# LayerNorm in one decoder layer: the variance by one 264-column product with the ones matrix, the inverse root on all copies, the last scalings in quarters

## The chip, the cores and the metric

The kernel runs on one NeuronCore of one Trainium2 chip. Its engines work side by side, each through a queue of its own in order: TensorE (PE) multiplies matrices, with its weight loads (PEld) listed beside it; VectorE (DVE) and ScalarE (ACT) do elementwise work; GpSimd (POOL) and SyncE (SP) do small jobs and issue DMAs. The metric is device time in microseconds (us), lower is better. Before the change it is 2132.67 us, the median of three runs (2131.72 to 2135.8).

## The reference

One layer with post-LayerNorm residuals over 1056 tokens (1024 of a prompt, 32 of samples), each with 1024 features:

```
h = LN1(alpha*x + 0.5*SwiGLU_a(x))
z = h @ w_in + b_in                      # attention, spatial gating and gates from z
h = LN2(alpha*h + (sigmoid(gA)*(A@w_oa) + sigmoid(gB)*(B@w_ob)) @ w_out)
y = LN3(alpha*h + 0.5*SwiGLU_b(h))

def layer_norm(x, g, b):
    mu = mean(x); var = mean((x - mu)**2)
    return (x - mu) * rsqrt(var + 1e-5) * g + b
```

All is float32. Only the three LayerNorms LN1, LN2 and LN3 are touched here. The kernel works with x/alpha in place of x, so its constant beside the variance is EPL = 1e-5/alpha^2.

## The kernel before

**Layout.** Activations lie transposed: a tile has 128 features on its partitions and tokens along its columns. The tokens are cut into four chunks of C = 264 columns, c0 to c3. A chunk of a LayerNorm's input is held in two tiles Y[c][0] and Y[c][1] of 4 x 264 columns (128x1056), so 8 feature blocks in all. A float32 product is done as three passes on split operands (high by high, high by low, low by high); all of them are issued from line 243, in the helper `mm3`.

**What comes into a norm.** Each feature block of a chunk is a residual sum that ends in a product of 12 passes (LN1 and LN3) or 24 passes (LN2) into one of three PSUM banks called mm. DVE evicts the bank and adds it to Y: line 1155 in LN1 and LN3 (function `out`), line 2025 in LN2 (function `mix`). A bank can be filled again only when DVE has evicted it; so TensorE is at most three blocks ahead of DVE.

**A norm of one chunk, before.** `center` takes the mean: line 761 multiplies the ones matrix (1/1024 everywhere, so the sum comes out on all 128 partitions) with a 264-column sum of the blocks, and line 767 subtracts it from the two tiles, 1056 columns each. `square_step` squares a block on ACT (line 806) and adds pairs on DVE (line 810). `norm` then does, for LN1, LN2 and LN3:

- line 816 adds the last two 264-column sums (DVE); line 819 brings the variance into a 128x3 tile, tokens on partitions: three products with one column each, weights the sums (PE, six passes in the trace);
- ACT takes the square root of the 128x3 tile (line 876); DVE the reciprocal and a Newton step (lines 877 to 880). For c3 of LN2 and c2 of LN3 all of it is done on DVE with three Newton steps (lines 867 to 872);
- after HOP[i] steps of the generator, line 833 spreads the result over all partitions: three products with the identity (PE, six passes);
- line 844 multiplies the two tiles by it (DVE, 128x1056 each), line 852 applies gain and bias (ACT, eight blocks of 264 columns; in c3 every second block is done by DVE, line 849). LN1 and LN2 then split the result into high and low parts (lines 254 and 255) for the next stage's products; LN3 sends it out by DMA (line 858).

**What sets the order.** A list scheduler places every instruction at build time, by priorities and by its own estimates of duration. Evictions and squares are marked `urgent` (300 places ahead). The norms are generators in a queue that `tick` advances after each block of products; `yield` and `pause(n)` hand back to it, so HOP sets after how many steps a norm goes on. Each engine then runs its list in that order, and a waiting instruction holds all behind it on its engine.

Of the kernel before, what the change touches and what calls it, by code (L numbers as in the profile page):

```python
# [12 lines left out]
F32 = mybir.dt.float32  # L13
F32R = mybir.dt.float32r
I32 = mybir.dt.int32
AF = mybir.ActivationFunctionType
ALU = mybir.AluOpType
# [4 lines left out]
P = 128  # L22
# [5 lines left out]
C = 264  # L28
NC = NT // C
KH = KB // 2  # L30
# [13 lines left out]
EPS = 1e-5  # L44
EPL = EPS / ALPHA**2
# [17 lines left out]
ROWS = 8  # L63
LATE = 16
MID = 3
HOP = (4, 1, 4)
WARM = 2
MAGIC = float(0x5F3759DF)
BOTH = mybir.DependencyInfo(mybir.DependencyClass.Sync, mybir.DependencyReason.DATA)
# [15 lines left out]
class Trunk:  # L85
# [631 lines left out]
    def consts(self):  # L717
        nc, a, cp = self.nc, self.a, self.cp
        self.ident = cp.tile([P, P], F32, name="ident")
        make_identity(nc, self.ident)  # L720
        self.eps = {}
        for e in (EPS, EPL):
            self.eps[e] = cp.tile([P, 1], F32, name=f"eps{len(self.eps)}")
            nc.vector.memset(self.eps[e], e)
        self.ones = cp.tile([P, P], F32, name="ones")
        nc.vector.memset(self.ones, 1.0 / D)
        self.cols = cp.tile([P, 98], F32, name="cols")
        nc.sync.dma_start(self.cols, a["cols"])
        self.qb = cp.tile([P, 6], F32, name="qb")
        nc.vector.tensor_scalar(self.qb, self.cols[:, 48:54], -0.125, None, op0=ALU.mult)  # L730
# [54 lines left out]
    def square_step(self, c, n, tail=False):  # L785

        nc = self.nc
        tt = nc.vector.tensor_tensor
# [3 lines left out]
        sq = self.sq  # L792
        if tail:
# [6 lines left out]
            else:  # L800
                with self.urgent():
                    tt(sq[:, 0], y, y, op=ALU.mult)
                    tt(s[:, 0], s[:, 0], sq[:, 0], op=ALU.add)
            return
        with self.urgent():
            nc.scalar.activation(sq[:, n % 2], y, AF.Square)
# [4 lines left out]

    def norm(self, c, i, mode, Y, s):
        nc = self.nc
        offs = (0, P, C - P)
        if mode != "out" or c < NC - 1:
            nc.vector.tensor_tensor(s[:, 0], s[:, 0], s[:, 1], op=ALU.add)
        pv = self.ax_tile()[:, :3]
        for j, o in enumerate(offs):
            nc.tensor.matmul(pv[:, j : j + 1], s[:, 0, o : o + P], self.ones[:, 0:1], start=True, stop=True)  # L819
        rt = self.X([P, 2, 3], "rs")  # L820
        r, t = rt[:, 0], rt[:, 1]
        if c == NC - 1 and i == 1 or c == NC - 2 and mode == "out":
            self.rsqrt_dve(r, t, self.X([P, 3], "rx", 1), pv, EPL)
        else:
            self.rsqrt(r, t, pv, EPL)
        if i == 1 and c == NC - 2:
            nc.scalar.activation(self.X([P, 2], "warm", 1)[:, :1], r[:, :1], AF.Silu)
        for _ in range(HOP[i]):
            yield
        pb = self.ax_tile()[:, :C]  # L830
        for j, o in enumerate(offs):
            lo = 0 if j < 2 else 2 * P - o
            nc.tensor.matmul(  # L833
                pb[:, o + lo : o + P], r[:, j : j + 1].to_broadcast([P, P]), self.ident[:, lo:], start=True, stop=True
            )
        yield
        while mode == "out" and c == NC - 2 and NC - 1 not in self.lns:
            yield
# [2 lines left out]
        cast = None  # L841
        for j in range(2):
            y = Y[j]
            nc.vector.tensor_tensor(y, y, pb.unsqueeze(1).to_broadcast([P, KH, C]), op=ALU.mult)  # L844
            for m in range(KH):
                n = KH * j + m
                g, b = self.vec(2 * i, n), self.vec(2 * i + 1, n)
                if c == NC - 1 and m % 2:
# [22 lines left out]
            tt(t, t, -0.5, r, op0=ALU.mult, op1=ALU.mult)  # L871
            self.chain = tt(r, t, 1.5, r, op0=ALU.add, op1=ALU.mult).ins

    def rsqrt(self, r, t, v, eps):
        tt = self.nc.vector.scalar_tensor_tensor
        self.nc.scalar.activation(r, v, AF.Sqrt, bias=self.eps[eps])
        self.nc.vector.reciprocal(r, r)
        tt(t, v, eps, r, op0=ALU.add, op1=ALU.mult)
        tt(t, t, -0.5, r, op0=ALU.mult, op1=ALU.mult)
        self.chain = tt(r, t, 1.5, r, op0=ALU.add, op1=ALU.mult).ins  # L880

    def start_ln(self, c, i, mode):
        g = self.norm(c, i, mode, self.Y[c], self.sqs[c])
# [1339 lines left out]
```

## Time and profile before

The profiled execution took 2133.41 us, with a span of 2130.2 us on the core; 3.2 us lie around the span. The median of the runs shown is 0.74 us below the profiled execution.

| what | value |
|---|---|
| median of three runs | 2132.67 us |
| profiled execution / its span | 2133.41 / 2130.2 us |
| PE busy | 2100.3 us (99%) |
| DVE busy | 1590.1 us (75%) |
| ACT busy | 935.4 us (44%) |
| granted TensorE clock, mean | 0.995 |

LN1 lies at about 650 to 702 us of the span, LN2 at about 1380 to 1490, LN3 at about 2040 to the end. A row of the timeline gives the start, the time to the end of the last of its instructions, engine, line, operation, the tile written and the tiles read, the number of instructions, and in brackets the idle time of the engine before it with what ended it. Since instructions of an engine overlap at their ends, the rate of a run of equal ones is read from the starts of two rows, not from one row's length. The rows of windows give: window, its length, then busy time (and count) of PE, PEld, DVE, ACT and POOL, then the granted clock, the DMA engines' mean busy share and GB/s.

### The profile page before, as it was taken

Reading aid. Unit: us, or ns where it says so; the run is one execution under the profiler, and the core shown is the slowest. Engines: PE = TensorE matmul, PEld = TensorE weight load, DVE = VectorE, ACT = ScalarE, POOL = GpSimd, SP = SyncE. Lnnn points to the kernel's source line nnn. Section 1 sums busy time; section 2 is a strip of 40 time slices with the busy share of each in tenths; the row PEclk is TensorE's granted clock in tenths of the full one; section 3 lists DMA queues with packets and bytes.
Section 4 is the critical chain, followed back from the end, with each engine's and each line's share of the span. In section 5 each row is a group of like instructions: output and inputs, shape, how many; then the busy total and the mean of one; then the engine's idle time right before and its main releaser. Section 6 shows DMA issues by size and latency. Waiting matters only on the chain.

```text
span 2130.2 us, 43357 instructions
## 1 busy us (share of the span) xinstructions
PE 2100.3 (99%) x17163; PEld 2066.2 (97%) x17163; DVE 1590.1 (75%) x2918; ACT 935.4 (44%) x1894; POOL 394.2 (19%) x374
## 2 busy tenths in 40 slices
PE   9999999999999999999999999999999999999997
PEld 8999999999999999999988889999999999999997
DVE  8877777766789846888767568787777777757787
ACT  5554454432224644434476543164545545512224
POOL 0234334300000022323001130000443333300000
PEclk9999999999999999999999999999999999999998
DMA  4365565499984336676855666332546545598752
GB/s 153 112 214 176 172 227 184 164 372 356 320 327 175 127 132 212 223 248 222 287 195 175 190 207 202 123 121 96 167 174 212 195 141 181 197 367 308 294 182 82
DMA packets 172187, 437.54 MB, mean 205 GB/s; under 512 B 23600, under 2 KB 58096, under 8 KB 169296
## 3 DMA queue, kind: packets, MB, share of 16 engines
q1 hardware_dynamic: 169568, 430.37, 57.3%
q0 software_dynamic: 1984, 3.87, 0.8%
q8 instruction: 134, 2.20, 0.4%
q10 hardware_dynamic: 432, 0.54, 0.1%
q14 instruction: 69, 0.57, 0.1%
HBM read 315.32 MB, written 165.57 MB: 226 GB/s over the span
## 4 chain that ended last, share of the span: by engine, by line
PE 95%; DVE 3%; DMA 1%; issue 1%; ACT 0%; POOL 0%; ACTq 0%; DVEq 0%
PE ax L243 51%; PE mm L243 39%; PE ax L1437 1%; PE ax L1487 1%; PE ax L1464 1%; DVE W L255 1%; DVE S L255 0%; DVE S L844 0%; DMA S<-cD 0%; PE ax L833 0%; PE mm L1860 0%; DMA S<-xc 0%; DVE S L767 0%; PE ax L1420 0%; PE ax L819 0%
## 5 line engine op out<-in xcount | busy, mean ns | idle before, releaser
L243 PE MATMUL ax<-S,W 128*128 128x264 f32 x7392 | 988.6, 284 | 1.8 <-DVE W L255 1.8
L243 PEld LDWEIGHTS ax<-S,W 128*128 128x128 f32 x7392 | 936.2, 188 | 2.6 <-DVE W L255 2.5
L243 PE MATMUL mm<-S,W 128*128 128x264 f32 x5232 | 735.8, 287 | 8.8 <-ACT S L254 2.7
L243 PEld LDWEIGHTS mm<-S,W 128*128 128x128 f32 x5232 | 674.1, 189 | 22.3 <-issue 6.5
L243 PE MATMUL mm<-S,S 128*128 128x264 f32 x1944 | 284.8, 285 | 3.8 <-DVE S L1155 2.4
L243 PEld LDWEIGHTS mm<-S,S 128*128 128x128 f32 x1944 | 255.3, 188 | 5.9 <-issue 2.3
L254 ACT CAST W<-R 128x512 fp32r<-128x512 f32 (+4 forms) x214 | 137.5, 658 | 230.8 <-DMA R<-w2pa 65.7
L255 DVE TENSOR_TENSOR W<-R,W 128x512 fp32r<-128x512 f32 (+4 forms) x214 | 178.3, 837 | 60.8 <-ACT W L254 59.1
L243 PE MATMUL ax<-S,S 128*128 128x264 f32 x1488 | 219.0, 284 | 0.2 <-DVE S L1048 0.2
L243 PEld LDWEIGHTS ax<-S,S 128*128 128x128 f32 x1488 | 196.7, 188 | 0.5 <-DVE S L1048 0.4
L255 DVE TENSOR_TENSOR W<-Q,W 128x512 fp32r<-128x512 f32 (+2 forms) x199 | 147.7, 759 | 56.8 <-ACT W L254 56.8
L254 ACT CAST W<-Q 128x512 fp32r<-128x512 f32 (+2 forms) x199 | 128.7, 678 | 106.6 <-DVE Q L393 104.5
L1048 DVE SCALAR_TENSOR_TENSOR S<-ax,S 128x264 f32<-128x264 f32 x240 | 99.4, 427 | 60.8 <-PE ax L243 59.6
L111 POOL CAST S<-ones 128x1 fp32r<-128x1 f32 x36 | 12.8, 364 | 583.5 <-PE ax L243 210.8
L612 ACT ACTIVATE S<-S 128x528 f32<-128x528 f32 x80 | 47.2, 638 | 135.6 <-DVE S L609 135.6
L446 POOL TENSOR_TENSOR Q<-R 128x512 f32<-128x512 f32 x36 | 47.4, 1315 | 200.9 <-DVE W L255 86.9
L474 POOL TENSOR_TENSOR Q<-R 128x256 f32<-128x256 f32 x20 | 20.7, 1034 | 344.2 <-DVE W L255 273.1
L255 DVE TENSOR_TENSOR S<-Q,S 128x1024 fp32r<-128x1024 f32 (+1 forms) x59 | 65.6, 1111 | 22.5 <-ACT S L254 22.4
L1264 ACT ACTIVATE S<-ax,cols 128x264 f32<-128x264 f32 (+5 forms) x99 | 40.3, 496 | 90.6 <-PE ax L243 86.3
L652 DVE TENSOR_TENSOR M<-M,M 128x264 f32<-128x264 f32 x60 | 63.4, 1082 | 11.7 <-ACT M L658 11.7
L254 ACT CAST S<-Q 128x1024 fp32r<-128x1024 f32 (+1 forms) x59 | 56.9, 965 | 31.9 <-DVE Q L404 29.0
L600 ACT COPY M<-ax 128x264 f32<-128x264 f32 x80 | 26.9, 376 | 95.0 <-issue 88.1
(269 smaller groups left out, 2326.4 us busy)
## 6 DMA issues: line engine op xcount, KB each, us to landing
ws<-st SPq DMA_DIRECT2D x144, 256.0 KB
S<-sumsA SPq DMA_DIRECT2D x63, 528.0 KB
S<-sumsB SPq DMA_DIRECT2D x63, 528.0 KB
R<-w13b SPq DMA_DIRECT2D x54, 512.0 KB
R<-w13a SPq DMA_DIRECT2D x52, 512.0 KB
M<-kv SPq DMA_DIRECT2D x96, 256.0 KB
sumsA<-M SPq DMA_DIRECT2D x90, 264.0 KB
sumsB<-M SPq DMA_DIRECT2D x90, 264.0 KB
```

Of the source, the lines that this page charges most:

```text
L243: mm = lambda a, b, s, e: nc.tensor.matmul(o, a[:, cc], b, start=s, stop=e, skip_group_check=True)
L254: a = self.nc.scalar.copy(hi, src)
L255: b = self.nc.vector.tensor_tensor(lo, src, hi.bitcast(F32), op=ALU.subtract)
L446: tt(s12[:, lo], cd[:, lo], cd[:, hi], op=ALU.add)
L600: go(one, 1, lambda x: copy(r[:, x], one[x]), True)
L612: nc.scalar.activation(h[:, x], h[:, x], AF.Silu)
L652: nc.vector.tensor_tensor(t, t, m, op=ALU.add)
L1048: nc.vector.scalar_tensor_tensor(y(x, r, e), bank[x], HALF, y(x, r, e), op0=ALU.mult, op1=ALU.add)
L1264: nc.scalar.activation(o, view(bank[x]), fn, bias=b, scale=sc)
L1437: m = nc.tensor.matmul(pS[h][:, r, :nk], q[e, i * P : (i + 1) * P], k[e, k0 : k0 + nk], start=True, stop=True)
L1464: nc.tensor.transpose(pT[r][:, h, o], s[:, r, h, o], self.ident)
L1487: nc.tensor.matmul(pv[0][e, (i % 4) * P : (i % 4 + 1) * P], V[:, i - (nb - 1) + b, e], sT[:, r, h, b * P : b * P + P], start=b == 0, stop= ...
```

## The change

For every norm but c3 of LN2, which keeps the way on 128x3 tiles (three products out, the root on DVE, three products back; now a function `narrow_root`):

- DVE forms -s0-s1 in place of s0+s1 (line 819 in the new numbering), and one product of the ones matrix with that 264-column tile gives minus the variance on all 128 partitions at once (line 820). The product back is gone.
- after HOP[i] steps, now (2, 1, 2) in place of (4, 1, 4), `wide_root` works on 128x264 elements: ACT takes the inverse root r of 4(var+EPL) from PSUM (line 870) and 4r^2 (line 871), DVE does two operations in place in PSUM (lines 874 and 875), a Newton step. LN2's c2 loads the Silu table behind it, as before (line 873).
- the scaling (now line 835) stands inside the loop over blocks; for c2 and c3 of LN3 it is done in four pieces of 128x528, each just ahead of the two blocks that read it, in place of two of 128x1056.
- one constant tile of 4*EPL takes the place of two.

```diff
@@ -63,7 +63,7 @@
 ROWS = 8
 LATE = 16
 MID = 3
-HOP = (4, 1, 4)
+HOP = (2, 1, 2)
 WARM = 2
 MAGIC = float(0x5F3759DF)
 BOTH = mybir.DependencyInfo(mybir.DependencyClass.Sync, mybir.DependencyReason.DATA)
@@ -718,10 +718,8 @@
         nc, a, cp = self.nc, self.a, self.cp
         self.ident = cp.tile([P, P], F32, name="ident")
         make_identity(nc, self.ident)
-        self.eps = {}
-        for e in (EPS, EPL):
-            self.eps[e] = cp.tile([P, 1], F32, name=f"eps{len(self.eps)}")
-            nc.vector.memset(self.eps[e], e)
+        self.eps = cp.tile([P, 1], F32, name="eps")
+        nc.vector.memset(self.eps, 4 * EPL)
         self.ones = cp.tile([P, P], F32, name="ones")
         nc.vector.memset(self.ones, 1.0 / D)
         self.cols = cp.tile([P, 98], F32, name="cols")
@@ -800,7 +798,9 @@
             else:
                 with self.urgent():
                     tt(sq[:, 0], y, y, op=ALU.mult)
-                    tt(s[:, 0], s[:, 0], sq[:, 0], op=ALU.add)
+                    nc.vector.scalar_tensor_tensor(
+                        s[:, 0], s[:, 0], -1.0, sq[:, 0], op0=ALU.mult, op1=ALU.subtract
+                    )
             return
         with self.urgent():
             nc.scalar.activation(sq[:, n % 2], y, AF.Square)
@@ -811,28 +811,15 @@
 
     def norm(self, c, i, mode, Y, s):
         nc = self.nc
-        offs = (0, P, C - P)
-        if mode != "out" or c < NC - 1:
-            nc.vector.tensor_tensor(s[:, 0], s[:, 0], s[:, 1], op=ALU.add)
-        pv = self.ax_tile()[:, :3]
-        for j, o in enumerate(offs):
-            nc.tensor.matmul(pv[:, j : j + 1], s[:, 0, o : o + P], self.ones[:, 0:1], start=True, stop=True)
-        rt = self.X([P, 2, 3], "rs")
-        r, t = rt[:, 0], rt[:, 1]
-        if c == NC - 1 and i == 1 or c == NC - 2 and mode == "out":
-            self.rsqrt_dve(r, t, self.X([P, 3], "rx", 1), pv, EPL)
+        if c == NC - 1 and i == 1:
+            pb = yield from self.narrow_root(s)
         else:
-            self.rsqrt(r, t, pv, EPL)
-        if i == 1 and c == NC - 2:
-            nc.scalar.activation(self.X([P, 2], "warm", 1)[:, :1], r[:, :1], AF.Silu)
-        for _ in range(HOP[i]):
-            yield
-        pb = self.ax_tile()[:, :C]
-        for j, o in enumerate(offs):
-            lo = 0 if j < 2 else 2 * P - o
-            nc.tensor.matmul(
-                pb[:, o + lo : o + P], r[:, j : j + 1].to_broadcast([P, P]), self.ident[:, lo:], start=True, stop=True
-            )
+            pb = self.ax_tile()[:, :C]
+            if mode != "out" or c < NC - 1:
+                nc.vector.scalar_tensor_tensor(s[:, 0], s[:, 0], -1.0, s[:, 1], op0=ALU.mult, op1=ALU.subtract)
+            nc.tensor.matmul(pb, self.ones, s[:, 0], start=True, stop=True)
+            yield from self.pause(HOP[i])
+            self.wide_root(pb, i == 1 and c == NC - 2)
         yield
         while mode == "out" and c == NC - 2 and NC - 1 not in self.lns:
             yield
@@ -841,8 +828,11 @@
         cast = None
         for j in range(2):
             y = Y[j]
-            nc.vector.tensor_tensor(y, y, pb.unsqueeze(1).to_broadcast([P, KH, C]), op=ALU.mult)
+            q = KH // 2 if mode == "out" and c >= NC - 2 else KH
             for m in range(KH):
+                if m % q == 0:
+                    e = y[:, m : m + q]
+                    nc.vector.tensor_tensor(e, e, pb.unsqueeze(1).to_broadcast([P, q, C]), op=ALU.mult)
                 n = KH * j + m
                 g, b = self.vec(2 * i, n), self.vec(2 * i + 1, n)
                 if c == NC - 1 and m % 2:
@@ -871,13 +861,38 @@
             tt(t, t, -0.5, r, op0=ALU.mult, op1=ALU.mult)
             self.chain = tt(r, t, 1.5, r, op0=ALU.add, op1=ALU.mult).ins
 
-    def rsqrt(self, r, t, v, eps):
-        tt = self.nc.vector.scalar_tensor_tensor
-        self.nc.scalar.activation(r, v, AF.Sqrt, bias=self.eps[eps])
-        self.nc.vector.reciprocal(r, r)
-        tt(t, v, eps, r, op0=ALU.add, op1=ALU.mult)
-        tt(t, t, -0.5, r, op0=ALU.mult, op1=ALU.mult)
-        self.chain = tt(r, t, 1.5, r, op0=ALU.add, op1=ALU.mult).ins
+    def wide_root(self, v, silu):
+
+        nc = self.nc
+        m = self.M([P, 2, C])
+        r, q = m[:, 0], m[:, 1]
+        tt = nc.vector.scalar_tensor_tensor
+        nc.scalar.activation(r, v, AF.Abs_reciprocal_sqrt, bias=self.eps, scale=-4.0)
+        nc.scalar.activation(q, r, AF.Square, scale=2.0)
+        if silu:
+            nc.scalar.activation(self.X([P, 2], "warm", 1)[:, :1], q[:, :1], AF.Silu)
+        tt(v, v, EPL, q, op0=ALU.subtract, op1=ALU.mult)
+        self.chain = tt(v, v, 3.0, r, op0=ALU.add, op1=ALU.mult).ins
+
+    def narrow_root(self, s):
+
+        nc = self.nc
+        nc.vector.tensor_tensor(s[:, 0], s[:, 0], s[:, 1], op=ALU.add)
+        offs = (0, P, C - P)
+        pv = self.ax_tile()[:, :3]
+        for j, o in enumerate(offs):
+            nc.tensor.matmul(pv[:, j : j + 1], s[:, 0, o : o + P], self.ones[:, 0:1], start=True, stop=True)
+        rt = self.X([P, 2, 3], "rs", 1)
+        r = rt[:, 0]
+        self.rsqrt_dve(r, rt[:, 1], self.X([P, 3], "rx", 1), pv, EPL)
+        yield
+        pb = self.ax_tile()[:, :C]
+        for j, o in enumerate(offs):
+            lo = 0 if j < 2 else 2 * P - o
+            nc.tensor.matmul(
+                pb[:, o + lo : o + P], r[:, j : j + 1].to_broadcast([P, P]), self.ident[:, lo:], start=True, stop=True
+            )
+        return pb
 
     def start_ln(self, c, i, mode):
         g = self.norm(c, i, mode, self.Y[c], self.sqs[c])
```

Old and new line numbers of the lines that stay: 1155 becomes 1170, 767 becomes 765, 761 becomes 759, 757/758 become 755/756, 844 becomes 835, 852 becomes 842, 849 becomes 839, 797 and 798/799 become 795 and 796/797, 802/803 become 800/801; 806, 810, 254 and 255 stay.

In the rows below S names tiles of activations or weights, M and X the middle-sized and small ones, mm and ax PSUM banks; the tile written stands left of the arrow. In LN1 the halves of c0, c1, c2, c3 are S_5567/S_5976, S_5697/S_5978, S_5569/S_5980, S_5699/S_5982 before, and after the change S_5565/S_5974, S_5695/S_5976, S_5567/S_5978, S_5697/S_5980.

**DVE in LN1, while c2's blocks come in.** Before, from the second of c2's evictions to its fifth:

```order
L1155 SCALAR_TENSOR_TENSOR S_5569<-mm_8540,S_5569 128x264
L816 TENSOR_TENSOR M_8330<-M_8330 128x264
L1155 SCALAR_TENSOR_TENSOR S_5569<-mm_8555,S_5569 128x264
L1155 SCALAR_TENSOR_TENSOR S_5569<-mm_8580,S_5569 128x264
L844 TENSOR_TENSOR S_5567<-S_5567,ax_8380 128x1056
L844 TENSOR_TENSOR S_5976<-S_5976,ax_8380 128x1056
L810 TENSOR_TENSOR M_8527<-M_8527,M_8569 128x528
L767 TENSOR_TENSOR S_5699<-S_5699,ax_8389 128x1056
L767 TENSOR_TENSOR S_5982<-S_5982,ax_8389 128x1056
L877 RECIPROCAL X_8534<-X_8534 128x3
L1155 SCALAR_TENSOR_TENSOR S_5980<-mm_8604,S_5980 128x264
```

The scaling of c0 (844) and the subtraction of c3's mean (767) stand between the fourth and the fifth. After, from the second mean subtraction of c2 on:

```order
L765 TENSOR_TENSOR S_5978<-S_5978,ax_8304 128x1056
L755 TENSOR_TENSOR M_8335<-M_7931 128x264
L255 TENSOR_TENSOR W_9304<-R_9265,W_9303 128x1024
L1170 SCALAR_TENSOR_TENSOR S_5976<-mm_8443,S_5976 128x264
L810 TENSOR_TENSOR M_8328<-M_8328,M_8378 128x528
L756 TENSOR_TENSOR M_8335<-M_8335,S_7395 128x264
L874 SCALAR_TENSOR_TENSOR ax_8330<-ax_8330,M_8352 128x264
L1170 SCALAR_TENSOR_TENSOR S_5976<-mm_8459,S_5976 128x264
L1170 SCALAR_TENSOR_TENSOR S_5567<-mm_8504,S_5567 128x264
L810 TENSOR_TENSOR M_8328<-M_8328,M_8425 128x528
L875 SCALAR_TENSOR_TENSOR ax_8330<-ax_8330,M_8352 128x264
L1170 SCALAR_TENSOR_TENSOR S_5567<-mm_8523,S_5567 128x264
```

and right behind these:

```order
L765 TENSOR_TENSOR S_5697<-S_5697,ax_8388 128x1056
L765 TENSOR_TENSOR S_5980<-S_5980,ax_8388 128x1056
L810 TENSOR_TENSOR M_8328<-M_8328,M_8457 128x528
L835 TENSOR_TENSOR S_5565<-S_5565,ax_8330 128x1056
L835 TENSOR_TENSOR S_5974<-S_5974,ax_8330 128x1056
L1170 SCALAR_TENSOR_TENSOR S_5567<-mm_8548,S_5567 128x264
```

The same four wide operations now stand two evictions earlier in c2, between its second (mm_8523) and third (mm_8548).

**PE at the same place.** Before, from the end of c2's fourth block:

```order
L243 MATMUL mm_8580<-S_8033,W_8130 128x264
L833 MATMUL ax_8380<-ident,X_8337 128x128 x2
L833 MATMUL ax_8380<-ident,X_8337 128x8
L761 MATMUL ax_8389<-M_8345,ones 128x264
L819 MATMUL ax_8530<-ones,M_8330 128x1 x3
L243 MATMUL mm_8604<-S_7955,S_8162 128x264
```

After, from the end of c2's second block:

```order
L243 MATMUL mm_8523<-S_8032,W_8078 128x264
L243 MATMUL mm_8523<-S_8031,W_8079 128x264
L759 MATMUL ax_8388<-M_8335,ones 128x264
L243 MATMUL mm_8548<-S_7953,W_8127 128x264
L243 MATMUL mm_8548<-S_7954,W_8127 128x264
```

The small products of 833 and 819 are gone from here; c3's mean product stands alone between two blocks. (A float32 product of the ones matrix or the identity is one row here and two matmuls in the trace.)

**ACT at the end of LN3.** S_23045/S_23452 are c2's halves and S_23175/S_23454 c3's before; S_22994/S_23401 and S_23124/S_23403 after. Before:

```order
L797 ACTIVATE M_26133<-S_23454 128x264
L876 ACTIVATE X_26170<-ax_26166,eps_165 128x3
L852 ACTIVATE S_23045<-S_23045,cols 128x264 x4
L852 ACTIVATE S_23452<-S_23452,cols 128x264 x4
L852 ACTIVATE S_23175<-S_23175,cols 128x264 x2
L852 ACTIVATE S_23454<-S_23454,cols 128x264 x2
```

After:

```order
L871 ACTIVATE M_25971<-M_25971 128x264
L795 ACTIVATE M_26054<-S_23403 128x264
L842 ACTIVATE S_22994<-S_22994,cols 128x264 x2
L870 ACTIVATE M_26091<-ax_26089,eps 128x264
L842 ACTIVATE S_22994<-S_22994,cols 128x264 x2
L842 ACTIVATE S_23401<-S_23401,cols 128x264 x2
L871 ACTIVATE M_26091<-M_26091 128x264
L842 ACTIVATE S_23401<-S_23401,cols 128x264 x2
L842 ACTIVATE S_23124<-S_23124,cols 128x264 x2
L842 ACTIVATE S_23403<-S_23403,cols 128x264 x2
```

Before, c3's root stands ahead of all of c2's gain-and-bias steps; after, its two ACT steps (870 and 871) stand behind two and behind six of them.

## The prediction

> **What bounds the kernel now.** I read the page's head and chain first, then windows over the three norms, then the timelines of those windows.
>
> ```profile
> span 2130.2 us, 43357 instructions
> PE 2100.3 (99%) x17163; PEld 2066.2 (97%) x17163; DVE 1590.1 (75%) x2918; ACT 935.4 (44%) x1894; POOL 394.2 (19%) x374
> PE 95%; DVE 3%; DMA 1%; issue 1%; ACT 0%; POOL 0%; ACTq 0%; DVEq 0%
> ```
>
> The chain that ended last is TensorE for 95%. Whatever leaves TensorE's list ought to shorten the end one for one, unless another engine is late just there. So the stages of the norms must be seen by themselves (LN1, a piece of LN2, LN3, the tail):
>
> ```profile
> 655.00:700.00 45.00, 42.48 (x340) 41.61 (x339) 42.23 (x77) 24.46 (x47) 0.00 (x0) 1.00 0.32 109
> 1380.00:1450.00 70.00, 70.00 (x579) 69.87 (x578) 58.62 (x97) 39.12 (x70) 1.72 (x6) 1.00 0.27 98
> 2060.00:2095.00 35.00, 34.85 (x281) 34.38 (x279) 30.55 (x57) 11.88 (x26) 0.00 (x0) 1.00 0.02 6
> 2115.00:2131.00 16.00, 2.92 (x18) 2.80 (x18) 7.89 (x18) 6.56 (x13) 0.00 (x0) 0.58 0.34 136
> ```
>
> In LN1 DVE is busy 42.23 of 45.00 us, and TensorE 42.48: two engines are at their limit, and TensorE already waits. In LN2 TensorE is busy throughout and DVE has 11 us free of 70. In LN3 DVE is at 87%. In the last 16 us TensorE hardly works: a serial tail.
>
> **What leaves TensorE.** The price of the small products stands between rows of the stream in LN2:
>
> ```profile
> 1427.45 11.13 PE L243 MATMUL mm<-S,W 128*128 128x264 f32 x90
> 1438.42 0.72 PE L819 MATMUL ax<-ones,M 128*128 128x1 f32 x6
> 1439.00 8.24 PE L243 MATMUL mm<-S,W 128*128 128x264 f32 x66
> 1447.08 0.73 PE L833 MATMUL ax<-ident,X 128*128 128x128 f32 x6
> 1447.67 24.31 PE L243 MATMUL mm<-S,W 128*128 128x264 f32 x198
> 655.52 0.60 PE L761 MATMUL ax<-M,ones 128*128 128x264 f32 x2
> 655.77 1.82 PE L243 MATMUL mm<-S,W 128*128 128x264 f32 x12
> ```
>
> Start to start, 90 passes take 10.97, so 0.122 each and 1.466 for a block of 12. Line 819 takes 1439.00 - 1438.42 = 0.58, line 833 0.59. The new product has the form of line 761, which takes 655.77 - 655.52 = 0.25 (two passes at 0.122). One norm loses 0.58 + 0.59 - 0.25 = 0.92. In the stream this counts for four chunks in LN1 (3.7), three in LN2 (2.8) and two in LN3 (1.8); of LN3's c2 only line 819 and the new product lie in the stream (0.34). Sum 8.6 us off TensorE.
>
> [...]
>
> **What it costs on DVE and ACT.** Out go a reciprocal and three 128x3 operations of 0.16; in come two operations of 128x264 on PSUM. On ACT a 128x3 root becomes two of 264 columns.
>
> ```profile
> L1048 DVE SCALAR_TENSOR_TENSOR S<-ax,S 128x264 f32<-128x264 f32 x240 | 99.4, 427 | 60.8 <-PE ax L243 59.6
> L806 ACT ACTIVATE M<-S 128x264 f32<-128x264 f32 x94 | 36.7, 419 | 65.8 <-DVE S L1155 31.5 <-DVE S L2025 22.5 <-DVE S L767 11.7
> L767 DVE TENSOR_TENSOR S<-S,ax 128x528 f32<-128x528 f32 x8 | 5.2, 697 | 0.1
> L876 ACT ACTIVATE X<-ax,eps 128x3 f32<-128x3 f32 x10 | 2.6, 259 | 5.9 <-PE ax L819 5.9
> ```
>
> In place in PSUM was not in the trace. Its nearest row, line 1048 (reads PSUM, 264 columns), gives 0.43, 0.35 from start to start; I take that, 0.16 as lower bound (the small operations) and 0.70 (twice the elements) as upper. DVE so gains a few tenths per norm and no more. The new ACT functions I price at line 806's 0.42 (bounds 0.26 and 0.84); ACT is busy 24.46 of LN1's 45 us and hides that.
>
> **LN1: the order counts more than the price.**
>
> ```profile
> 675.24 0.61 PE L761 MATMUL ax<-M,ones 128*128 128x264 f32 x2
> 676.04 2.40 DVE L767 TENSOR_TENSOR S<-S,ax 128x1056 f32<-128x1056 f32 x2
> 678.37 1.21 DVE L255 TENSOR_TENSOR W<-R,W 128x1024 fp32r<-128x1024 f32 x1
> 685.07 0.73 PE L833 MATMUL ax<-ident,X 128*128 128x128 f32 x6
> 685.65 0.69 PE L761 MATMUL ax<-M,ones 128*128 128x264 f32 x2
> 685.84 2.42 DVE L844 TENSOR_TENSOR S<-S,ax 128x1056 f32<-128x1056 f32 x2
> 686.18 0.72 PE L819 MATMUL ax<-ones,M 128*128 128x1 f32 x6
> 688.17 0.70 DVE L810 TENSOR_TENSOR M<-M,M 128x528 f32<-128x528 f32 x1
> 688.79 2.41 DVE L767 TENSOR_TENSOR S<-S,ax 128x1056 f32<-128x1056 f32 x2
> 691.20 0.74 DVE L1155 SCALAR_TENSOR_TENSOR S<-mm,S 128x264 f32<-128x264 f32 x2
> 691.66 1.73 PE L243 MATMUL mm<-S,S 128*128 128x264 f32 x12 [0.29 <-DVE S L1155]
> ```
>
> Before, DVE does 5.4 us without an eviction (685.84 to 691.20: scaling 2.33, sums 0.62, mean 2.41). TensorE has cover: 1.70 us of small products (685.07 to 686.77) and three free banks, 4.4. It waits 0.29 at 691.66. After, the same 5.4 us stand two evictions earlier, and the cover is one mean product (0.25) and 4.4. Even a punctual DVE (the eviction of mm_8523 0.05 after its block, the first of the new order 0.43 behind the pile) leaves 0.05 + 0.35 + 5.4 + 0.48 - 4.65 = 1.6 us of stall.
>
> DVE is not punctual. In the new order it begins c2's subtraction at about 675.9 and ends it at 678.3; by the rows' spacing there follow one sum for the mean (0.35), one split (1.14, its 1.21 less the overlap), three evictions (1.05), two sums of squares (1.24), the mean's other sum (0.35) and the two root operations (0.7): mm_8523 comes at 683.1. TensorE, no longer held by line 819, has four blocks done from 675.7 on at 675.7 + 4 x 1.466 = 681.6. So DVE is 1.4 late: **a stall of 3.0** (bounds 1.6, with DVE on time, and 3.7, with the root's operations at their upper 0.70). Of it 0.29 was there before, and c3's mean product, which took 0.53 ahead of line 819 (685.65 to 686.18), takes 0.25. The two following scalings, and the gates behind c3's norm (ACT's list there holds two table loads), I put at 0.6 and 0.5: DVE stays full, so a scaling of 2.4 with evictions on both sides (0.8) meets a cover of 4.65 only when it is on time; bounds 0 and 2.0. LN1: 3.7 + 0.3 + 0.3 - 3.0 - 1.1 = **0.2 gained**; by the bounds from 1.4 lost (3.7 of stall, 2.0 behind it) to 2.7 gained (1.6 and nothing).
>
> **LN2.** A block has 24 passes, 2.9 us, so three banks cover 8.8 and a pile of 5.4 passes unseen. Gain 2.8.
>
> **LN3.**
>
> ```profile
> 2090.37 2.42 DVE L844 TENSOR_TENSOR S<-S,ax 128x1056 f32<-128x1056 f32 x2 [0.82 <-PE ax L833]
> 2092.71 2.41 DVE L767 TENSOR_TENSOR S<-S,ax 128x1056 f32<-128x1056 f32 x2
> 2095.04 1.10 DVE L1155 SCALAR_TENSOR_TENSOR S<-mm,S 128x264 f32<-128x264 f32 x3
> 2095.52 4.03 PE L243 MATMUL mm<-S,S 128*128 128x264 f32 x31 [0.66 <-DVE S L1155]
> ```
>
> Before, the same two jobs stood together and cost 0.66. After, DVE's list has evictions between c0's scaling and c3's mean, so I take 0.5 of it back, and 0.3 for mean products that no longer stand ahead of line 819. The work is 1.8 + 0.3 = 2.1: **2.9** in all, 1.8 if a pile of the new list costs what the old did and a little more, 3.3 if the whole 0.66 and all four mean slots go.
>
> **The tail.** What counts from TensorE's last block on:
>
> ```profile
> 2111.27 3.42 PE L243 MATMUL mm<-S,S 128*128 128x264 f32 x26
> 2114.74 0.42 DVE L1155 SCALAR_TENSOR_TENSOR S<-mm,S 128x264 f32<-128x264 f32 x1
> 2118.45 4.09 ACT L852 ACTIVATE S<-S,cols 128x264 f32<-128x264 f32 x8 [0.33 <-DVE S L844]
> 2120.82 1.42 PE L833 MATMUL ax<-ident,X 128*128 128x128 f32 x6 [3.00 <-DVE X L880]
> 2122.28 2.42 DVE L844 TENSOR_TENSOR S<-S,ax 128x1056 f32<-128x1056 f32 x2 [1.60 <-PE ax L833]
> 2124.61 1.39 DVE L849 TENSOR_SCALAR S<-S,cols 128x264 f32<-128x264 f32 x4
> ```
>
> TensorE ends at T = 2114.7, the last scaling begins at T + 7.6, the last DVE work ends at T + 11.3, and the output is out 4.2 later (2130.2). After: the last sum of squares ends at T + 2.4, the product begins at 2.5, c2's quarters fill DVE to 4.9. On ACT c3's root stands behind two steps of c2 (0.5 each, from 3.0) and begins at 4.0; then four more (to 6.45), and only then line 871, to 6.9. DVE stands idle from 4.9 to 6.9, does its two operations (0.9) and four quarters (0.62 each, to 10.4), and its last four blocks to 11.7: **0.4 lost**, from 1.5 lost (ACT's new functions at 0.84, a slower product) to 1.0 gained (c2's steps earlier).
>
> **Sum.** 0.2 + 2.8 + 2.9 - 0.4 = 5.5, of 8.6 us that leave TensorE. Against the profiled execution's 2133.41 that is 2127.9; the median of the runs lies 0.74 below it, so **2127.2**. With every bound on its good side the sum is 2.7 + 2.8 + 3.3 + 1.0 = 9.8 (2122.9), on its bad side -1.4 + 2.8 + 1.8 - 1.5 = 1.7 (2131.0).
>
> **The rivals.**
>
> *All of it comes through.* If DVE catches up before the pile in LN1 (a scheduler's order is no time), 8.6 + 0.5 + 0.6 less the tail's 0.4 gives 9.3: 2123.4. For it: the chain's 95% on TensorE, and the old pile cost 0.29 only. Against it: DVE at 94% in LN1. [...] 0.22.
>
> *DVE eats more.* LN3's DVE is at 87%; if piles there cost as in LN1 and LN1 ends 1.0 down, 2.8 + 1.0 - 1.0 - 0.4 leaves 2.4: 2130.3, no change. 0.2.
>
> *Slower.* The root now passes ACT twice and DVE twice. On DVE line 874 holds all behind it until line 871 is done, and 871 stands in ACT's list behind squares that wait for DVE's evictions. Where DVE comes to 874 early, each norm can cost a square (0.42), 871 (0.42) and two hand-overs, 1.5 to 1.9; at the seven norms of LN1 and LN3 this is up to 13. Then 13 + 0.4 - 8.6 = 5 lost, 2137.5. It decides where DVE has less than some 1 us of other work between 870 and 874. Against it: in the new list sums and evictions stand between, and ACT is half idle. 0.08.
>
> **How the numbers follow.** Forecast 0.5, the rivals 0.22, 0.2 and 0.08. Range 2122.0 to 2131.0: the two ends of the sum, and one us more below, where the first rival's 2123.4 may itself come out better; the slower rival is left out, and some of the edges of the others. The forecast's own range is 2124.5 to 2129.5. A measurement of this kernel can tell about 0.2%, 4.3 us, so faster means below 2128.4: four fifths of the forecast (0.4) and the first rival (0.22), together 0.62. Within 0.2%: the rest of the forecast and the second rival, 0.3. Slower, above 2136.9: 0.08.
>
> **What would show it.** In the timeline of LN1 a wait of about 3 us of line 243 for line 1170, right behind four wide DVE operations, where 0.29 stood; none over 0.3 in LN2; in LN3 the 0.66 smaller; rows of line 820 with 0.25 to the next row; line 874 with no idle time ahead of it but in the tail, where about 2 us stand ahead of the last one; PE's busy time lower by about 9. Waits ahead of 874 in LN1 and LN3 would make the slower rival right; a stall under 1 us in LN1 the first one.

## The result

The changed kernel takes 2127.36 us (median of 14 runs, 2125.31 to 2129.91), the kernel before 2132.64 (14 runs, 2129.24 to 2135.8): a ratio of 0.9976 with a 95% interval of 0.9968 to 0.9984. That is 5.3 us less, 0.25% (3.4 to 6.8 us by the interval). The forecast was 2127.2.

The head of the page and the chain, after the change:

```profile
span 2123.5 us, 43110 instructions
PE 2092.9 (99%) x17053; PEld 2057.1 (97%) x17053; DVE 1590.0 (75%) x2892; ACT 939.6 (44%) x1906; POOL 394.8 (19%) x374
PE 93%; DVE 3%; DMA 1%; ACT 1%; issue 1%; POOL 0%; ACTq 0%; DVEq 0%
```

TensorE's busy time fell by 7.4 us (2100.3 to 2092.9); DVE's did not move (1590.1 and 1590.0), as the small operations that left it and the two wider ones that came nearly cancel (a second profile of the kernel before has 1585.5, so differences of a few us say nothing here). ACT now holds 1% of the chain, where it had 0%.

The span of this one profiled execution is 6.7 us shorter than that of before (2123.5 and 2130.2), more than the medians are apart. To see where, TensorE's rows serve as marks: the first mean product of LN1, the first identity product behind LN1, the first mean products of LN2 and LN3, and TensorE's end. Before:

```profile
655.52 0.60 PE L761 MATMUL ax<-M,ones 128*128 128x264 f32 x2
784.19 0.38 PE L1683 MATMUL ax<-ident,S 128*32 128x128 f32 x2
1364.43 0.61 PE L761 MATMUL ax<-M,ones 128*128 128x264 f32 x2
2066.69 0.61 PE L761 MATMUL ax<-M,ones 128*128 128x264 f32 x2
```

and after:

```profile
656.05 0.60 PE L759 MATMUL ax<-M,ones 128*128 128x264 f32 x2
785.08 0.38 PE L1698 MATMUL ax<-ident,S 128*32 128x128 f32 x2
1363.16 0.61 PE L759 MATMUL ax<-M,ones 128*128 128x264 f32 x2
2062.00 0.61 PE L759 MATMUL ax<-M,ones 128*128 128x264 f32 x2
2110.10 1.22 PE L820 MATMUL ax<-M,ones 128*128 128x264 f32 x2 [2.45 <-DVE M L801]
```

The last row gives TensorE's end: 2110.10 - 2.45 = 2107.65; before it was 2114.69. The differences:

| stage | before | after | gained | forecast |
|---|---|---|---|---|
| up to LN1 | 655.52 | 656.05 | -0.5 | 0 |
| LN1 and the gates behind it | 128.67 | 129.03 | -0.4 | 0.2 |
| attention and mixing, up to LN2 | 580.24 | 578.08 | 2.2 | 0 |
| LN2 and the feed-forward stage, up to LN3 | 702.26 | 698.84 | 3.4 | 2.8 |
| LN3, up to TensorE's end | 48.00 | 45.65 | 2.4 | 2.9 |
| tail | 15.51 | 15.85 | -0.3 | -0.4 |

The bound between the last two of LN2 and LN3 is a mean product that the new list also shifts by 0.6 us (five passes more stand behind it), so these two are best taken together: 5.8 gained, 5.7 forecast. The first and the third line belong to no norm; the runs below take them up.

**LN1 after the change.** The timeline of PE and DVE where the wide operations stand:

```profile
682.46 0.61 PE L759 MATMUL ax<-M,ones 128*128 128x264 f32 x2
683.51 0.42 DVE L1170 SCALAR_TENSOR_TENSOR S<-mm,S 128x264 f32<-128x264 f32 x1
683.85 2.41 DVE L765 TENSOR_TENSOR S<-S,ax 128x1056 f32<-128x1056 f32 x2
686.17 0.70 DVE L810 TENSOR_TENSOR M<-M,M 128x528 f32<-128x528 f32 x1
686.79 2.41 DVE L835 TENSOR_TENSOR S<-S,ax 128x1056 f32<-128x1056 f32 x2
689.12 1.11 DVE L1170 SCALAR_TENSOR_TENSOR S<-mm,S 128x264 f32<-128x264 f32 x3
689.60 4.84 PE L243 MATMUL mm<-S,S 128*128 128x264 f32 x25 [2.14 <-DVE S L1170]
694.28 0.61 PE L820 MATMUL ax<-M,ones 128*128 128x264 f32 x2
```

The stall that was forecast is there: 2.14 us of line 243 waiting for line 1170, right behind four wide DVE operations (683.85 to 689.12). But look at the row itself: its 25 passes take 694.28 - 689.60 = 4.68 us, 0.187 each, where the kernel's stream has 0.122 (90 passes in 10.97 us in the prediction's rows of LN2). The windows of the stall and of the piece behind it (granted clock in the third column from the right) say why:

```profile
686.73:690.14 3.41, 1.27 (x10) 1.06 (x10) 3.41 (x6) 2.07 (x4) 0.00 (x0) 1.00 0.00 0
690.14:693.55 3.41, 3.41 (x18) 3.41 (x17) 2.03 (x4) 3.24 (x7) 0.00 (x0) 0.50 0.40 159
```

In the second window TensorE is busy all the time, but at a granted clock of 0.50. The stall cost not 2.1 us but 2.1 + (4.68 - 25 x 0.122) = 3.8. Nothing in the prediction had that.

**The new operations.** Between the start of a new product and that of the next row lie 0.25 us (694.53 - 694.28):

```profile
694.28 0.61 PE L820 MATMUL ax<-M,ones 128*128 128x264 f32 x2
694.53 1.70 PE L243 MATMUL mm<-S,S 128*128 128x264 f32 x11
696.06 6.00 PE L243 MATMUL mm<-S,W 128*128 128x264 f32 x48
```

But this is not its whole price. The 11 passes behind it take 1.53 from start to start, where 11 x 0.122 is 1.34: by the starts of the single passes, the first one behind the product takes 0.32, the others 0.12. So the product costs 0.25 + 0.19 = 0.44. The part on the prediction comes back to this. DVE's two operations in place in PSUM cost 0.435 each, as the row chosen for them (0.427):

```profile
L870 ACT ACTIVATE M<-ax,eps 128x264 f32<-128x264 f32 x11 | 5.3, 478 | 13.0 <-PE ax L820 12.9
L874 DVE SCALAR_TENSOR_TENSOR ax<-ax,M 128x264 f32<-128x264 f32 x11 | 4.8, 435 | 3.5 <-ACT M L871 3.5
L871 ACT ACTIVATE M<-M 128x264 f32<-128x264 f32 x11 | 4.6, 416 | 0.0
```

Over all 11 norms line 874 waited 3.5 us for line 871: 2.00 in the tail, 1.07 in LN2, 0.41 in LN3. Outside the tail no wait of TensorE follows from it.

**The tail after the change**, from T = 2107.65 on:

```profile
2110.61 1.10 ACT L842 ACTIVATE S<-S,cols 128x264 f32<-128x264 f32 x2 [3.48 <-DVE S L835]
2111.62 0.46 ACT L870 ACTIVATE M<-ax,eps 128x264 f32<-128x264 f32 x1
2111.98 2.09 ACT L842 ACTIVATE S<-S,cols 128x264 f32<-128x264 f32 x4
2113.97 0.41 ACT L871 ACTIVATE M<-M 128x264 f32<-128x264 f32 x1
2114.42 0.44 DVE L874 SCALAR_TENSOR_TENSOR ax<-ax,M 128x264 f32<-128x264 f32 x1 [2.00 <-ACT M L871]
2115.37 2.55 DVE L835 TENSOR_TENSOR S<-S,ax 128x528 f32<-128x528 f32 x4
2117.83 1.39 DVE L839 TENSOR_SCALAR S<-S,cols 128x264 f32<-128x264 f32 x4
```

Line 870 begins at T + 3.97 (forecast 4.0), line 871 ends at T + 6.7 (6.9), line 874 waits 2.00 us behind it, and DVE ends at T + 11.6 (11.7).

### The profile page after: what moved, and what is told of

Read it like the earlier page. It is cut to its first block, busy times and chain, and to the rows that moved or that the text cites. A ratio compares the mean times of both kernels' runs of the same rounds, so it can differ in the third digit from the quotient of the medians.

```text
span 2123.5 us, 43110 instructions
## 1 busy us (share of the span) xinstructions
PE 2092.9 (99%) x17053; PEld 2057.1 (97%) x17053; DVE 1590.0 (75%) x2892; ACT 939.6 (44%) x1906; POOL 394.8 (19%) x374
## 4 chain that ended last, share of the span: by engine, by line
PE 93%; DVE 3%; DMA 1%; ACT 1%; issue 1%; POOL 0%; ACTq 0%; DVEq 0%
PE ax L243 50%; PE mm L243 39%; PE ax L1452 1%; PE ax L1502 1%; PE ax L1479 1%; DVE W L255 1%; DVE S L255 1%; DMA S<-sumsA 1%; ACT S L842 0%; PE mm L1875 0%; DMA S<-cD 0%; DMA S<-xc 0%; DVE S L765 0%; PE ax L1435 0%; DVE S L835 0%
```

## The experiments

Stages are named as in the table above. "The middle" is attention and mixing.

**The two kernels once more.** The first question is whether the middle's 2.2 us belong to the change.

> The changed kernel once more, nothing edited. Stages by TensorE's rows: LN1 from its first mean product to the first identity product of the stage behind (before 128.7 us, after 129.0), the middle from there to LN2's first mean product (580.2 and 578.1), the tail from TensorE's last L243 (15.5 and 15.85). Theory: LN1's loss is fixed by the order, so the stall of 2.1 us and the granted clock near 0.5 behind it come again, and LN1 is 129.0 within 0.3; the 2.1 us that the middle gained are waits for loaded data and not the change, so they differ by 0.5 us or more in this execution. Rival: the middle's gain is the change's; then it is 578.1 within 0.3 again.

> The kernel before once more, nothing edited. Theory: LN1 128.7 within 0.3, with the stall of 0.3 and a clock of 1.0; the middle's waits (1.23 us ahead of the product of line 1437 and 1.69 us in the mixing stage) are other ones, so that the middle differs from 580.2 by 0.5 us or more. Rival (the middle belongs to the order of the instructions): 580.2 within 0.3.

Measured: the changed kernel again 2127.7 us, with LN1 129.73, the middle 581.20, the tail 15.84; the kernel before again 2129.62 us, with LN1 128.57, the middle 579.11, the tail 15.55. So the middle of the change was once 2.2 shorter and once 1.0 longer than the first profile of before, and before itself differs by 1.1 between two executions. In the twelve profiles of this study (nine kernels, two of them more than once) it lies between 578.1 and 581.9 without regard to the edit; the time up to LN1, between 652.9 and 657.1, varies alike. Its waits are of this kind; the rows are from the first profile of before, and the waits in the changed kernel again were 0.91 and 2.06 at the same two places:

```profile
1211.47 1.13 PE L1437 MATMUL ax<-S,S 64*128 64x128 f32 x8 [1.23 <-DVE X L1447]
1261.45 4.15 PE L243 MATMUL mm<-S,W 128*128 128x264 f32 x32 [1.69 <-DVE W L255]
```

The DVE work ahead of the first waits for a load (5.12 us of idle time for DMA S<-cD, by DVE's rows). The middle's gain is thus not the change's, and the 6.7 us between the spans of the first pair of profiles is the change's share plus luck. The other stages repeat: LN2 with LN3 gives 744.49, 744.50 (change) and 750.26, 750.30 (before), the tail agrees within 0.04. LN1 does not: it was to be 129.0 within 0.3 and is 129.73, mostly because the wait for the gates at its end was 0.32 in the one and 0.90 in the other. In the changed kernel again the stall of LN1 is 2.14 once more, with the clock at 0.71 over the 3.6 us behind it (0.57 in the first).

**HOP back at (4, 1, 4).**

```diff
-HOP = (2, 1, 2)
+HOP = (4, 1, 4)
```

> The change with HOP back at (4, 1, 4). In its list DVE's scaling of c0 stands two evictions behind the subtraction of c3's mean; but the means of c2 and c3 now have one eviction between them. Theory (the place of the wide operations sets the stall, and the stall the clock): the stall of 2.1 us behind c0's scaling is gone, one of 1.0 to 1.6 stands behind the two means; if the clock only falls behind the longer one, LN1 is 126.5 to 127.5, else 128.5. Rival (the root's extra work on DVE and ACT costs LN1 what it costs, wherever it stands): LN1 129.0 within 0.3. LN3 and the tail within 0.5 of the changed kernel.

Measured: 2129.91 us; LN1 131.75, LN3 46.22, the tail 15.14. By LN1's sum the expectation missed, on the high side; LN3 (0.6 longer than in the changed kernel) and the tail (0.7 shorter) missed their bound of 0.5 too. By place it held: where c2's and c3's means now stand close together there is a stall of 1.05 with the clock at 1.0 behind it, and none behind c0's scaling. What made LN1 longer stands before and after these:

```profile
662.84 4.68 PE L243 MATMUL mm<-S,S 128*128 128x264 f32 x24 [1.91 <-DVE S L1170]
686.00 3.15 PE L243 MATMUL mm<-S,W 128*128 128x264 f32 x24 [1.05 <-DVE S L1170]
725.05 15.14 PE L243 MATMUL mm<-S,S 128*128 128x264 f32 x112 [2.45 <-ACT M L1239]
```

At 662.84, ahead of LN1's first root, a known stall of 1.47 is one of 1.91: ACT's cast of a weight tile, which waits for its load, begins at 657.06 where the changed kernel's first profile has 655.93, and DVE's work behind it comes later. The same stall is 1.70 in the third profile of the changed kernel below, so it varies without an edit. Behind it 24 passes took 4.68 us here, where the changed kernel's first profile has 3.15. At 725.05 the gates wait 2.45 where they had waited 0.32: the gain-and-bias steps that stand ahead of ACT's table loads (720.09 and 721.89 in the changed kernel's first profile, 1.28 us each) wait for a scaling that DVE now begins 2.3 us later in the span (714.85 for 712.58). Over the 3.6 us behind these two waits the granted clock is 0.53 and 0.60, behind the one of 1.05 it is 1.0.

**All mean subtractions in four pieces.**

```diff
-            self.mid.append(self.center(c, hs, 3 if c else 5, means[c], 1 if c else 2))
+            self.mid.append(self.center(c, hs, 3 if c else 5, means[c], 2))
```

> The change, with the mean subtractions of c1 to c3 in LN1 and LN3 in four pieces of 128x528 too. In the list that comes of it no four wide operations of LN1 stand together: the longest stretch without an eviction is 4.1 us by the rows' spacing, under the 4.65 of three banks and a mean product. Theory: no stall over 0.8 from c2 on, the clock stays at 1.0, LN1 is 125.3 to 126.5 (2.1 of stall and some 1.7 of slow clock less, up to 1.0 of small waits more). Rival: 129.0 within 0.3, with the stall at another place.

Measured: 2137.88 us; LN1 134.86, LN3 47.51, the tail 16.03. A miss: slower than before. No four wide operations stood together, but the smaller piles still cost 0.47, 0.79 and 1.17 of stall from c1 on; LN3 got a stall of 1.21 (line 243 for line 1170) that it had not had; and the early wait came to 2.17 with a clock of 0.55 behind it, that for the gates to 2.55 with 0.55. More pieces did not make the list better. They moved more than themselves: by DVE's rows c2's mean now stands three evictions earlier in LN1, c3's where it stood, and c0's scaling four later.

**Only c0's scaling later.** The cleanest separation: the generator of c0's norm is held for 18 steps ahead of the scaling.

```diff
             self.wide_root(pb, i == 1 and c == NC - 2)
+        if i == 0 and c == 0:
+            yield from self.pause(18)
         yield
```

DVE's list in LN1 is then that of the change up to the subtraction of c3's mean; from its second half on it reads (835 and 1170 are 837 and 1172 here)

```order
L765 TENSOR_TENSOR S_5980<-S_5980,ax_8375 128x1056
L810 TENSOR_TENSOR M_8328<-M_8328,M_8441 128x528
L1172 SCALAR_TENSOR_TENSOR S_5567<-mm_8519,S_5567 128x264
L837 TENSOR_TENSOR S_5565<-S_5565,ax_8330 128x1056
L1172 SCALAR_TENSOR_TENSOR S_5567<-mm_8540,S_5567 128x264
L837 TENSOR_TENSOR S_5974<-S_5974,ax_8330 128x1056
```

so that c2's evictions stand ahead of each half of c0's scaling.

> The change, with c0's scaling in LN1 held back for 18 more steps of its generator, and nothing else moved by hand. In the list that comes of it two evictions stand between and behind c0's two scaling halves; c3's mean subtraction stands alone. Theory (the four wide operations together make the stall, the stall makes the slow clock): the stall of 2.1 us shrinks under 0.7, the granted clock stays at 1.0 behind it, and LN1 is 125.0 to 126.5 where the changed kernel had 129.0 and 129.7; up to 2 more if the gates behind the norm wait longer, since c1 to c3 are scaled later. Rival (the root's price makes the stall wherever it stands): LN1 129 or more, with waits of 2 us in all at other places.

Measured: 2124.16 us; LN1 126.55. The whole list of TensorE's waits of 0.25 us or more in LN1 is now

```profile
662.22 3.17 PE L243 MATMUL mm<-S,S 128*128 128x264 f32 x24 [1.47 <-DVE S L1172]
670.99 1.73 PE L243 MATMUL mm<-S,W 128*128 128x264 f32 x12 [0.76 <-DVE S L1172]
720.92 19.34 PE L243 MATMUL mm<-S,S 128*128 128x264 f32 x157 [1.45 <-ACT M L1241]
```

The first two stood there before the change as well. The stall of 2.14 and the slow clock are gone (the granted clock is 1.00 over 655 to 700 us, where the changed kernel's first profile has 0.96); the same operations at the same price do not hold TensorE when evictions stand between them. The gates wait 1.1 us longer (1.45 for the changed kernel's 0.32), as the expectation allowed for. LN1 is 2.5 and 3.2 shorter than in the changed kernel's two profiles, and 2.1 shorter than before the change. So the rival that the root's price makes the stall is out.

**LN1 in the old way.** The change everywhere but in LN1, where the norm is that of before (with HOP 4):

```diff
-        if c == NC - 1 and i == 1:
+        if i == 0:
+            pb = yield from self.narrow_root(s, True)   # square root on ACT, then as before
+        elif c == NC - 1 and i == 1:
             pb = yield from self.narrow_root(s)
```

> The change with LN1's norms done in the old way (three products, the square root of 128x3 on ACT, the Newton step on DVE, three products back, HOP 4), so that LN1's list is that of the kernel before. Theory: LN1 is 128.6 within 0.3, with the stall of 0.3 and a clock of 1.0, so the change gains nothing in LN1 and loses up to 1; the stage from LN2's to LN3's first mean product stays at 698.8, the one from there to TensorE's end at 45.65. Rival (LN1 gains from the change, and other stages hide it): LN1 is over 129.7.

Measured: 2124.54 us; LN1 128.69 with a stall of 0.29 and nothing slow behind it (the granted clock is 1.00 over 655 to 700 us), LN2 up to LN3 698.95, LN3 45.72, the tail 15.74. LN1, its stall and clock, and both stages are as expected. The change gains nothing in LN1; all of its gain is in LN2 and LN3.

**The tail: line 871 right behind line 870.** c3's root is issued ahead of c2's last scalings, and c2's gain-and-bias steps from the third on wait for it in ACT's list:

```diff
+        last = mode == "out" and c == NC - 2
+        if last:
+            for _ in range(HOP[i] + 1):
+                next(self.lns[NC - 1])
...
-                    with self.tc.issue_after(cast) if cast else ExitStack():
+                    first = self.root if last and n > 1 else cast
+                    with self.tc.issue_after(first) if first else ExitStack():
```

(`self.root` is the instruction of line 871.)

> The change, with the second ACT step of c3's root in LN3 (line 871) right behind the first, ahead of the other six gain-and-bias steps of c2. Theory: DVE's idle time of 2.0 us ahead of the last line 874 goes, ACT's last step ends at about T + 9.8 and the tail is 14.1 (13.8 to 14.6) where it is 15.85. Rival (the tail's length is the wide root's own: a product on a slow clock, two ACT and two DVE operations): the tail stays at 15.5 to 15.9. All other stages as in the changed kernel, the middle apart.

Measured: 2122.77 us; the tail 14.42, LN1 128.97, LN2 up to LN3 698.85, LN3 45.65. The timeline, from T = 2106.48:

```profile
2110.45 0.46 ACT L875 ACTIVATE M<-ax,eps 128x264 f32<-128x264 f32 x1
2110.94 0.42 ACT L876 ACTIVATE M<-M 128x264 f32<-128x264 f32 x1
2111.27 5.08 ACT L847 ACTIVATE S<-S,cols 128x264 f32<-128x264 f32 x10
2111.39 0.44 DVE L879 SCALAR_TENSOR_TENSOR ax<-ax,M 128x264 f32<-128x264 f32 x1
```

(lines 875, 876, 847 and 879 here are 870, 871, 842 and 874 of the change.) DVE's wait of 2.00 is gone, ACT works without a gap to T + 9.9, and the tail loses 1.43. The rival, that the wide root itself is too long, is out: it is where its second step stands.

**The quarters undone.**

```diff
-            q = KH // 2 if mode == "out" and c >= NC - 2 else KH
+            q = KH
```

> The change with the last scalings of LN3 in halves of 128x1056, as before it. Theory: the place of line 871 sets the tail, not the size of the pieces: c2's four gain-and-bias steps stand ahead of it (2.0 us) as six steps did, line 874 waits until about T + 6.8, and the tail is 15.9 (15.6 to 16.2). Rival (the quarters are worth what they cut off the first piece, twice 0.6 us): 16.8 to 17.2.

Measured: 2128.64 us (with LN1 at 130.53 and the middle at 581.11, neither of them touched by the edit); the tail 15.01. Both expectations missed, on the other side: without quarters the tail is 0.84 shorter. The rows, from T = 2111.89:

```profile
2115.12 0.48 ACT L870 ACTIVATE M<-ax,eps 128x264 f32<-128x264 f32 x1 [3.76 <-PE ax L820]
2115.50 2.09 ACT L842 ACTIVATE S<-S,cols 128x264 f32<-128x264 f32 x4
2117.49 0.41 ACT L871 ACTIVATE M<-M 128x264 f32<-128x264 f32 x1
2117.93 0.44 DVE L874 SCALAR_TENSOR_TENSOR ax<-ax,M 128x264 f32<-128x264 f32 x1 [1.41 <-ACT M L871]
```

With halves the first of c2's steps is ready later, so line 870 stands first in ACT's list: it begins at T + 3.23 (3.97 with quarters), and four steps stand between it and line 871, not four and two ahead. Line 874 begins at T + 6.04 (6.77). I had taken the earlier start of 870 for granted with both and counted only the steps behind it. The quarters by themselves made the change 0.8 us slower: they gave ACT something to do ahead of c3's root.

In this run LN1 has its early stall at 2.11 with a clock of 0.53 over the 3.6 us behind it, and then the pile's 2.14 without one: the clock is 1.00 over the 3.6 us behind that. From LN1 to the end of LN3 it is the only stall over 1.8 us of this study that drew none; the last section sets its rows beside those of the changed kernel.

**Both edits together, timed.**

> The change with both edits: c0's scaling in LN1 held back for 18 steps, and c3's second ACT step of the root in LN3 ahead of c2's other six steps. Theory (two separate losses of the change, one in LN1's order, one in the tail's): LN1 126.5, tail 14.4, no stall over 1.8 us in LN1 and a clock of 1.0 there; against the changed kernel 2.5 to 3.2 and 1.4 less, 3.9 to 4.6 in all, so 2123 (2121.5 to 2124.5) where the changed kernel has 2127.4, and a ratio to the kernel before near 0.9955. Rival (the two edits do not add, since a TensorE that is earlier only waits for the middle's loaded data): 2125 or more.

> The changed kernel, unedited, timed beside the one above on the same chip: 2127.4 within 1.0; LN1 129.0 to 129.8 by its profile, tail 15.85.

Measured on one chip: both edits 2121.9 us (5 runs, 2121.67 to 2124.09), the changed kernel 2127.15 (11 runs, 2124.16 to 2129.4), the kernel before 2131.35 (15 runs); ratios to before 0.996 (0.9948 to 0.9973) and 0.9978 (0.9969 to 0.9987). LN1 is 126.55 and the tail 14.42 in the one, 130.07 and 15.88 in the other; the wait for the gates in the latter is 1.15, which with a clock of 0.64 behind the stall of 2.14 makes LN1 longer than the 129.8 that I had allowed. The two edits add: 5.25 us by the medians, of which the two stages of these profiles show 3.5 + 1.5 = 5.0. This version beats both kernels: 9.5 us less than before on this chip.

## Why the prediction was right

The time came out 0.2 us from the forecast. The places and kinds of gain and loss are the predicted ones; that the number is so near is in part luck. LN1, with 0.2 of gain forecast, lost 0.4, 1.1 and 1.4 us in the three profiles of the changed kernel; with 5.8 in LN2 and LN3 and 0.3 lost in the tail these stages give 4.1 to 5.1 us, where the forecast was 5.5 and the medians are 5.3 apart (3.4 to 6.8 by the interval). By its own steps:

**What leaves TensorE: right in the rows, one pass short in the price.** The spacings that the step used hold in every norm (0.58 to 0.59 for a group of six small products before, 97 to 98 ns each; 0.25 for a lone product). What it left out is the first pass behind a product: 0.32 behind a product of 264 columns, 0.205 behind a group of six small ones, 0.122 within the stream. The new list has the first at 21 places of the three norms, where the old one had it at 9, and the second at 2 where the old one had 17. So the passes behind them take back 0.4 us in LN1 and 0.7 in LN2 with LN3, a term that the sum does not have. LN2 with LN3 still gained 5.8 (two profiles each way, 0.05 apart) for 2.8 + 2.9, because other terms were too small: the old stall of LN3 gave 0.3 more than was taken, and the mean products that no longer stand ahead of a small one 0.15 more; for another 0.3 no row here accounts.

**The price of the root on DVE and ACT: right.** 0.435 for 0.43; on ACT 0.478 and 0.416 for 0.42.

**LN1: right in sum in the first profile, wrong in its terms.** The step said: a stall of 3.0, then 0.6 for c1's scaling and later ones and 0.5 for the gates, together 4.1 of loss. Measured in the first profile: the stall 2.14, no wait at any later scaling, the gates 0.32; and a term that the sum did not have, 1.6 us of slow clock behind the stall. Together 4.1. The stall was over-sized because DVE came to mm_8523's eviction only 1.05 behind that block (683.51 against 682.46; the step had 1.4, and its own 683.1 and 681.6 are 1.5 apart), TensorE being later there than I had reckoned, and because TensorE ran 5.0 us on its three banks and the mean product, not 4.65 (0.2 of it in the pass behind the product). It is within the bounds (1.6 to 3.7). The runs show the cause: with evictions between the wide operations both the stall and the slow clock are gone (LN1 126.55), and with LN1's old list it is 128.69. Even so, the 3.7 + 0.3 + 0.3 that LN1 was to gain, less 2.14, 1.6 and 0.32, is 0.2, and LN1 lost 0.4; in the kernel with c0's scaling later the same sum (4.3 - 1.45) lacks 0.7. Of what is lacking, 0.6 and 0.7, the passes behind the lone products are 0.4, and the wait for the gates costs 0.16 more by the starts of the passes than the idle time that its row lists; the rest, 0.1 or less in the one and 0.2 in the other, is open. In the second and third profiles the gates waited 0.90 and 1.15, and the third one's loss of 1.4 is the step's lower bound.

**LN2: right.** No wait over 0.25 in it.

**LN3: right in sum.** The old stall of 0.66 (0.8 by the starts of the passes) is gone altogether; I had taken 0.5 of it.

**The tail: right in place and size**, 0.33 lost for 0.4, and by the step named: line 871 stuck behind six steps of c2. What the prediction did not see is that the quarters, which looked like a help, are what put two of these steps ahead of line 870; without them the tail would have been 0.5 shorter than before the change.

**The rivals.** "All of it comes through" fell with the 2.14 us stall; it would have needed evictions between the wide operations, and the edit that puts them there gains 2.5 to 3.5 in LN1. "DVE eats more" fell with LN3, where no pile formed in the new list; it did form with the means in pieces (a stall of 1.21). Its other half, LN1 1.0 down, came true in two of the three profiles. "Slower" fell with line 874: waits of 1.07 in LN2 and 0.41 in LN3 that held no bank up, none in LN1.

**What was to show it.** Of the signs, the stall in LN1, the spacing of line 820 and the 2.00 us ahead of the last line 874 came as written; TensorE's busy time fell by 7.4, not 9, and the 1.6 us more that LN1's slow passes took are counted as busy; and line 874 had the two small waits outside the tail that it was not to have.

## What to carry to other kernels

Work taken off the engine that bounds a kernel came through here where the engine that hands it its buffers had slack (LN2 with LN3, 5.8 us), and not where that engine was full (LN1, 0.4 to 1.4 us lost; DVE was busy for 41.16 of the 45 us from 655 on): there the place of the long operations between the evictions decides, and the place is read from the instruction lists of both kernels, not from the prices. Ask of a stall not only how long it is but at what clock TensorE runs after it. Read the price of a small product up to the second pass behind it, not to the first (0.44 and 0.25 us here). And cutting the last work into smaller pieces helps only if the chain that ends the program moves forward with it; look at what the pieces put ahead of that chain on each engine.

## What the runs showed of the hardware

The stall of 2.14 us in the changed kernel's first profile cost 3.8, nearly twice its length. Over the twelve profiles, from LN1 to the end of LN3, TensorE waited 23 times for 1.2 to 1.74 us: the granted clock over the 3.6 us behind each was 1.00. It waited 14 times for 1.83 to 2.55 us, and 13 times the clock behind was 0.50 to 0.71. The same 24 passes show the price: in the kernel before they take 3.15 us behind a wait of 1.47, and with HOP at (4, 1, 4) they take 4.68 behind one of 1.91 (the row at 662.84 above). That is 0.44 us more of waiting and 1.53 more for the passes.

The length of a wait does not tell all of it. The stall of 2.14 us behind the wide operations of LN1 has a clock of 0.57, 0.71 and 0.64 over the 3.6 us behind it in the three profiles of the changed kernel; with the quarters undone it is as long, and the clock is 1.00 during it and behind it:

```profile
686.83:690.25 3.42, 2.50 (x21) 2.29 (x19) 3.42 (x5) 0.30 (x1) 0.00 (x0) 1.00 0.00 0
690.25:693.66 3.41, 2.19 (x18) 2.19 (x19) 2.55 (x6) 3.32 (x7) 0.00 (x0) 1.00 0.22 90
693.66:697.07 3.41, 3.41 (x29) 3.34 (x28) 2.17 (x4) 3.32 (x8) 0.00 (x0) 1.00 0.48 194
```

In the changed kernel's first profile all of the 2.14 us of idle time lies in one such row (686.73:690.14 above), and the next row is the slow one; here two rows share it, 0.92 and 1.22. No run sets the two cases apart by an edit, so what makes the difference is not shown.
